# Ranking eight experts on the chip, and giving three of them 64 slots with hi and lo in one product's rows

## The chip, the cores and the metric

The kernel runs on one core of one Trainium2 chip. Its time is the device time of one execution in microseconds; the kernel before took 1813.16 us (median of 3 runs, 1811.98 to 1815.05). A core has five engines that run side by side, each through its own instructions in order: TensorE (PE in the profile; PEld are its weight loads), VectorE (DVE), ScalarE (ACT), GpSimd (POOL) and SyncE (SP), which here starts the transfers. They wait for each other by semaphores.

## The reference

The whole computation is two blocks of a network on 256 tokens of 1024 features, in float32: four mixers and a feed-forward, four mixers and a mixture of experts, a linear recurrence with feed-forward, a sparse attention with feed-forward. The change lies in the mixture of experts. Cut to what is computed:

```python
def _swiglu(h, w1, w3, w2):
    return (jax.nn.silu(h @ w1) * (h @ w3)) @ w2

def _moe_ffn(h, router, w1, w3, w2):       # h [1, 256, 1024], 8 experts of 1408 hidden features
    xt = h.reshape(T, D)
    logits = (xt @ router).astype(jnp.float32)
    top_logit, top_idx = lax.top_k(logits, TOP_K)          # TOP_K = 2
    gates = jax.nn.softmax(top_logit, axis=-1)
    ...                                    # sort by expert, evaluate blocks of rows
        yb = _swiglu(xb, w1[e], w3[e], w2[e])
    ...                                    # sum back to the tokens, times the gate
```

Of the 512 assignments the eight experts hold, for the inputs that are timed, 59, 68, 57, 76, 47, 73, 70 and 62.

## The kernel before

**Products in two parts.** Every product of float32 values is made of three passes: a value is cut into a rounded part (hi) and the rest (lo), and x·w is taken as hi·hi + lo·hi + hi·lo. For weights this is done in `piece` (L391 to L425): SP loads a piece of 128x2048 (1 MB) into one of three `raw` buffers or, while the experts run, one of `MORE` = 6 further ones (`mraw`), L401; per part of 128x1024 ScalarE casts hi (`whi`, L422) and VectorE subtracts (`wlo`, L423). The rings of `whi` and `wlo` hold three parts each (`NHL`); a part's slot comes free when TensorE has used it. Both instructions are put into the program with high priority, so that they stand ahead of other work of the engine that is written at the same place.

**The experts.** `moe` (L1163) runs once, after the second block's mixers. It makes the router's logits (L1202; the router's columns padded to 128), cuts the normalized tokens into hi and lo with tokens on partitions (`token_split`, L652), chooses two of eight per token (L1208 to L1220), counts each token's place among its expert's tokens (`pos`, L1226), and builds for two experts at a time a 0/1 matrix `G` of tokens by slots (L1272). `gather` (L1280) multiplies the tokens with it: `ehi` and `elo`, features on partitions, 128 slots for each of two experts. `slots` (L1287) makes the slot's weight and 1/rms (`gs`) and the transpose of `G` (`GT`). An expert (`expert`, L1320) has its slots on the rows of a result: chunks of 512, 512 and 384 hidden features, for each w1 and then w3 (`tmaj`, L459, 8 steps of the contraction, three products each), silu (ScalarE, L1331), product with the gate (VectorE, L1334), a transpose on TensorE (L626) and a cut into `ghi` and `glo` (L651, L652). W2 takes its pieces two steps of the contraction at a time with both halves of the features (L1373 to L1375), except in the last expert, where it goes a half of the features at a time. Then the result is weighted and cut (L1346, L1347), spread over the tokens by `GT` (scatter, L1354 and L1355, 16 products of 256 columns) and added to the residual `x` (L549).

**Order.** The program is written as a sequence; a scheduler places each engine's instructions from it, and weights' loads and splits run ahead as far as buffers allow. Experts come in the order 0 to 7 with weights at fixed addresses. The gather for the next two experts is written ahead of experts 1, 3 and 5. At the end the largest count is read into a register; if it is over 128, a second pass runs all experts on the tokens beyond. For these inputs it isn't run.

Of the kernel before, what the change touches and what calls it, by code (L numbers as in the profile page):

```python
# [8 lines left out]
F32 = mybir.dt.float32  # L9
# [52 lines left out]
class Pack:  # L62
    """Small vectors side by side in one [128, n] array."""
# [103 lines left out]
def layout(inp, phases):  # L167
    """DRAM arrays of the launch, from the inputs by name."""
# [28 lines left out]
    rt = np.zeros((P, KD, P), np.float32)  # L197
    rt[:, :, :8] = g["router"][0].reshape(KD, P, 8).transpose(1, 0, 2)
    ev.add("router", rt.reshape(P, KD * P))
# [57 lines left out]
    for j in range(2):  # L257
        w[f"c1{j}"] = _chunk_fm(g["cmp_w1_2"][j], [np.arange(256)], [8, 8])
    for e in range(8):
        w1, w3 = g["moe_w1"][0, e], g["moe_w3"][0, e]  # L260
        pc = []
        for c_ in _cols(1408, 512):
            pc += _chunk_fm(w1, [c_], [4, 4]) + _chunk_fm(w3, [c_], [4, 4])
        w[f"m13{e}"] = pc
        w[f"m2{e}"] = (_chunk_fm(g["moe_w2"][0, e], [np.arange(D)], [2, 2, 2, 2, 2, 1]) if e < 7
                      else _chunk_fm(g["moe_w2"][0, e], _cols(D, 512), [4, 4, 3]))
    for k, pieces in w.items():
# [4 lines left out]
        a["W" + k] = arr  # L272
# [3 lines left out]
# --------------------------------------------------------------------------  # L276
# the program
# --------------------------------------------------------------------------

class Prog:  # L280
# [35 lines left out]
    def keep_busy(self, n):  # L316
        """products that nobody reads, where TensorE would wait so long that its clock is halved"""
# [4 lines left out]
    def late(self):  # L322
        """the constants that are not needed at once, behind the first weights"""
# [60 lines left out]
    def prefetch(self, w):  # L384
        """start loading the first weights of the next phase, ahead of a branch"""
# [777 lines left out]
    def moe(self, after):  # L1163
# [64 lines left out]
        for q in range(2):  # L1228
            token_split(q, pts[q])
# [556 lines left out]
```

## Time and profile before

| what | value |
|---|---|
| median of 3 runs (lowest, highest) | 1813.16 us (1811.98, 1815.05) |
| profiled execution, first to last instruction | 1810.8 us |
| mean granted clock of TensorE | 0.992 |
| PE busy | 1762.0 us (97%), 11443 instructions |
| DVE busy | 1452.2 us (80%), 2129 |
| ACT busy | 1174.3 us (65%), 1716 |
| POOL busy | 91.7 us (5%), 133 |
| read from HBM | 357.92 MB, 198 GB/s over the span |
| experts' first product, last scatter | 750.34 us, 1159.7 us |

The profile is one execution. Its span runs from the first to the last instruction; the runs' times are taken apart from it and also hold what lies around the span, and the profiled execution's own time is not listed beside it. A share of the whole span mixes phases with different limits, so the rows further down are of the experts' stretch alone. A matmul's length is modelled, so the step from one start to the next tells the pace of a row of products.

### The profile page before, as it was taken

To read this page: it belongs to the slowest core of one execution; us is meant where nothing else is said; L and a number is where in the kernel's file an instruction comes from. 1 tells how busy PE (TensorE), PEld (TensorE's weight loads), DVE (VectorE), ACT (ScalarE), POOL (GpSimd) and SP (SyncE) were. 2 spreads that over 40 slices of the span, in tenths; PEclk is the share of its full clock that TensorE was granted. 3 is DMA by queue.
4 is the path that set the end of the run, shared out by engine and by line. 5 is a ranking of instruction groups with operands and counts; after the bars stand their busy time and mean duration, and the time that the engine had idled before them with its cause. 6 is when DMAs were issued, how large, how long until landed. Compare 5 with 4: busy or idle time off the path is not lost. (4 is left out here: it accounts for less than half of the span.)

```text
span 1810.8 us, 29243 instructions
## 1 busy us (share of the span) xinstructions
PE 1762.0 (97%) x11443; PEld 1566.2 (86%) x11443; DVE 1452.2 (80%) x2129; ACT 1174.3 (65%) x1716; POOL 91.7 (5%) x133
## 2 busy tenths in 40 slices
PE   8999999999999999999999999888999998999999
PEld 7888998888978899888888888788888987788888
DVE  6789787886678977789989899788887589878774
ACT  6765556554566654687887877675655477766552
POOL 1100000000110010000000000031000022000000
PEclk9999999999999999999999999998999999999999
DMA  7323555555532265789989899434555555035553
GB/s 288 130 71 117 187 187 185 186 180 190 198 132 79 100 212 176 294 315 359 354 305 353 312 360 345 162 125 150 186 186 177 197 203 177 2 101 192 193 181 126
DMA packets 53777, 360.93 MB, mean 199 GB/s; under 512 B 6112, under 2 KB 6496, under 8 KB 15744
## 3 DMA queue, kind: packets, MB, share of 16 engines
q1 hardware_dynamic: 52848, 355.57, 55.4%
q0 software_dynamic: 640, 3.38, 0.5%
q8 instruction: 92, 1.51, 0.3%
q14 instruction: 53, 0.43, 0.1%
q10 hardware_dynamic: 144, 0.04, 0.0%
HBM read 357.92 MB, written 1.05 MB: 198 GB/s over the span
## 5 line engine op out<-in xcount | busy, mean ns | idle before, releaser
L423 DVE TENSOR_TENSOR wlo<-raw,whi 128x1024 fp32r<-128x1024 f32 (+3 forms) x465 | 546.2, 1178 | 214.1 <-ACT whi L422 187.3
L422 ACT CAST whi<-raw 128x1024 fp32r<-128x1024 f32 (+3 forms) x470 | 474.8, 1013 | 357.2 <-PE lin L457 110.0
L423 DVE TENSOR_TENSOR wlo<-mraw,whi 128x1024 fp32r<-128x1024 f32 (+1 forms) x185 | 216.7, 1193 | 19.7 <-ACT whi L422 11.8
L422 ACT CAST whi<-mraw 128x1024 fp32r<-128x1024 f32 (+1 forms) x185 | 189.4, 1029 | 46.7 <-PE lin L482 25.9
L456 PE MATMUL lin<-x,whi 128*128 128x256 f32 x736 | 197.3, 289 | 6.3 <-ACT whi L420 6.3
L457 PE MATMUL lin<-x,whi 128*128 128x256 f32 x736 | 198.9, 291 | 0.0
L568 PE MATMUL lin<-x,whi 128*128 128x512 f32 x576 | 156.8, 393 | 0.0
L454 PE MATMUL lin<-x,wlo 128*128 128x256 f32 x736 | 150.9, 288 | 0.4 <-DVE wlo L423 0.3
L456 PEld LDWEIGHTS lin<-x,whi 128*128 128x128 f32 x736 | 142.9, 194 | 7.7 <-ACT whi L420 6.3
L482 PE MATMUL lin<-whi,ehi 128*128 128x512 f32 (+1 forms) x384 | 144.5, 376 | 0.0
L457 PEld LDWEIGHTS lin<-x,whi 128*128 128x128 f32 x736 | 143.1, 194 | 1.5 <-issue 0.8
L482 PE MATMUL lin<-whi,elo 128*128 128x512 f32 (+1 forms) x384 | 144.0, 375 | 0.0
L568 PE MATMUL mx<-x,whi 128*128 128x512 f32 x480 | 129.7, 392 | 0.0
L454 PEld LDWEIGHTS lin<-x,wlo 128*128 128x128 f32 x736 | 115.4, 193 | 3.8 <-issue 2.5
L568 PEld LDWEIGHTS lin<-x,whi 128*128 128x128 f32 x576 | 104.6, 189 | 15.7
L482 PE MATMUL lin<-wlo,ehi 128*128 128x512 f32 (+1 forms) x384 | 114.7, 376 | 0.0
L568 PEld LDWEIGHTS mx<-x,whi 128*128 128x128 f32 x480 | 87.3, 189 | 13.3
L577 PEld LDWEIGHTS lin<-x,wlo 128*128 128x128 f32 x576 | 86.0, 190 | 8.1
L577 PE MATMUL lin<-x,wlo 128*128 128x256 f32 x576 | 88.8, 282 | 0.0
L482 PEld LDWEIGHTS lin<-whi,ehi 128*128 128x128 f32 x384 | 72.2, 188 | 10.8 <-ACT sa L1331 0.4
L482 PEld LDWEIGHTS lin<-whi,elo 128*128 128x128 f32 x384 | 72.2, 188 | 10.0
L482 PEld LDWEIGHTS lin<-wlo,ehi 128*128 128x128 f32 x384 | 70.7, 188 | 9.9
(605 smaller groups left out, 3882.0 us busy)
## 6 DMA issues: line engine op xcount, KB each, us to landing
mraw<-Wm SPq DMA_DIRECT2D x79, 1024.0 KB, 6.5
raw<-Wf SPq DMA_DIRECT2D x60, 1024.0 KB, 4.9
raw<-Ww_gate SPq DMA_DIRECT2D x32, 1024.0 KB, 4.9
raw<-Wffn SPq DMA_DIRECT2D x30, 1024.0 KB, 4.8
raw<-Ww_in SPq DMA_DIRECT2D x25, 1024.0 KB, 5.0
raw<-Wm SPq DMA_DIRECT2D x24, 1024.0 KB, 7.4
raw<-Wm SPq DMA_DIRECT2D x24, 768.0 KB, 5.2
raw<-Ww_branch SPq DMA_DIRECT2D x8, 1024.0 KB, 4.9
```

The lines of the kernel that those rows point to most:

```text
L422: (nc.gpsimd.tensor_copy if f & 1 else nc.scalar.copy)(hi[:, :kc * n], src)
L423: (nc.gpsimd if f & 2 else nc.vector).tensor_tensor(lo[:, :kc * n], src, hi[:, :kc * n].bitcast(F32), op=ALU.subtract)
L454: nc.tensor.matmul(o, lo[:, k, fs], xhi[:, kk, :], start=False, stop=end and k == kc - 1)
L456: nc.tensor.matmul(o, hi[:, k, fs], xhi[:, kk, :], start=kk == 0 and f % 2 == 0, stop=False)
L457: nc.tensor.matmul(o, hi[:, k, fs], xlo[:, kk, :], start=False, stop=False)
L482: nc.tensor.matmul(o, (xlo if i == 2 else xhi)[:, kk, ts], (lo if i == 1 else hi)[:, k, :], start=kk + i == 0, stop=last and (k, i) == ste ...
L568: mm = lambda f=f, k=k, kk=k0 + k: nc.tensor.matmul(banks[f], hi[:, k, f * P:(f + 1) * P], x2[:, kk].rearrange("p i t -> p (i t)"), start= ...
L577: nc.tensor.matmul(banks[f][:, 0:S], lo[:, k, f * P:(f + 1) * P], x2[:, k0 + k, 0], start=False, stop=False)
```

## The change

- The 128 slots of an expert become 64 for three of the positions 1, 3 and 5 of the order in which experts are run (`CAP`). Position 0 is always expert 0. The other seven are ranked by their counts of tokens on the chip; the three with fewest go to positions 1, 3 and 5, the others by rank to 2, 4, 6 and 7 (`RANKS`).
- The ranking is a chain of small VectorE operations behind `pos`; `ordered` brings positions and gates into the new order. Seven register loads on SP give the experts' numbers, from which the addresses of w13 and W2 are made.
- A small expert (`small_expert`) holds its tokens' hi in rows 0 to 63 and lo in rows 64 to 127 of one stationary tile. `both` multiplies it with a part's hi and lo, two products where there were three, and the halves of the result are added: a copy of the lower rows on ScalarE (L1448) and an addition on VectorE (L1449). Its W2 and scatter go the same way.
- W2 of every expert goes a half of the features at a time, in pieces of 4, 4 and 3 steps; `MORE` is 7; the router has 64 columns; the gather's copies and `GT` are made per expert.
- The second pass runs if any expert has more tokens than its position has slots.

The lines taken out and put in, without those that only rename or drop comments:

```diff
-RAW, NHL, SUB, MORE = 3, 3, 1024, 6
+RAW, NHL, SUB, MORE = 3, 3, 1024, 7
+HALF = 64
+RANKS = (-1, 0, 3, 1, 4, 2, 5, 6)
+CAP = tuple(HALF if 0 <= r < 3 else P for r in RANKS)
...
-        pl = self.bank("mx").rearrange("p (t e) -> p t e", e=P)
+        pl = self.bank("mx")[:, 0:P].rearrange("p (t e) -> p t e", e=HALF)
...
+        cn = T([8], "cn")
+        nc.vector.tensor_copy(cn, pcn[:, 0:8])
+        g7, e7 = T([7, 7], "g7"), T([7, 7], "e7")
...
+        nc.vector.tensor_tensor(g7, ne, nj, op=ALU.is_gt)
+        nc.vector.tensor_tensor(e7, ne, nj, op=ALU.is_equal)
+        nc.vector.tensor_mul(e7, e7, v("jlte").rearrange("p (e j) -> p e j", e=8)[:, 1:8, 1:8])
+        nc.vector.tensor_add(g7, g7, e7)
+        rk = T([7], "rk")
+        nc.vector.tensor_reduce(rk, g7, axis=AX.X, op=ALU.add)
+        oh = T([7, 7], "oh")
+        nc.vector.tensor_tensor(oh, rk.unsqueeze(1).to_broadcast([P, 7, 7]),
+                                v("rkp").unsqueeze(2).to_broadcast([P, 7, 7]), op=ALU.is_equal)
...
+        pos_e, pos = pos, T([2, 8], "poso")
+        ordered(pos, pos_e)
+        ixf, ixi = T([7], "ixf"), T([7], "ixi", 1, I32)
...
+        order = [nc.values_load(ixi[0:1, p:p + 1], engines=(mybir.EngineType.SP,), min_val=1, max_val=7)
+                 for p in range(7)]
+        W13 = [a["Wm13"][0]] + [a["Wm13"][bass.ds(r, 1)].rearrange("a g p n -> (a g) p n") for r in order]
...
                 for d2 in range(4):
...
-                        (nc.vector.tensor_copy if e2 == 0 and src is hlo else nc.scalar.copy)(o, pt)
+                        for i in range(2):
+                            e = 2 * e2 + i
+                            dst = rows[e][0]
+                            n = slice(HALF * q, HALF * (q + 1)) if half[e] else slice(0, P)
+                            o = dst[0 if half[e] else q][:, 2 * d2:2 * d2 + 2, n]
+                            (nc.vector.tensor_copy if e2 == 0 and q else nc.scalar.copy)(o, pt[:, :, i, n])
...
-        with self.tc.If(reg > P):
-            experts(P)
+        with self.tc.If(reg > 0):
+            experts(True)
...
+    def both(self, w, first, kgroups, n, x2, sink):
...
+        for k0, kc, hi, lo in parts:
+            for i, src in enumerate((hi, lo)):
                 for k in range(kc):
...
+                    nc.tensor.matmul(bank, x2[:, k0 + k], src[:, k, :], start=k0 + k + i == 0,
+                                     stop=i == 1 and k0 + k == nk - 1)
+        sink(bank)
...
+    def small_expert(self, w13, w2, x2, gs, GT, last):
...
+        g2 = T([11, P], "ghi", 1, F32R)
+        up, dn = slice(0, HALF), slice(HALF, P)
+        rs = gs[up, 1:2]
...
+        def total(out, o):
+            nc.scalar.copy(out, o[dn])
+            nc.vector.tensor_tensor(out, o[up], out, op=ALU.add)
+        for ci, n in enumerate((512, 512, 384)):
+            sa, sb = T([512], "sa", 2)[up, :n], T([512], "sa", 2)[up, :n]
...
+            def sink_a(o):
+                total(sa, o)
+                nc.scalar.activation(sa, sa, AF.Silu, scale=rs)
...
+            def sink_b(o):
+                total(sb, o)
+                nc.vector.scalar_tensor_tensor(sa, sb, rs, sa, op0=ALU.mult, op1=ALU.mult)
...
+                self.split(g2[:, sl, up], g2[:, sl, dn], pt)
+            self.both(w13, 4 * ci, [4, 4], n, x2, sink_a)
+            self.both(w13, 4 * ci + 2, [4, 4], n, x2, sink_b)
```

In the rows below a line of the changed kernel is 5 higher than that of the same code before (L423 is L428, L626 is L631).

VectorE where the experts begin, before: cnt is the rank of a logit in its token, sel the choice, pos the places, x_1090 the tokens' lo.

```order
L1218 TENSOR_TENSOR gt_7832<-gt_7832,eq_7833 128x128
L652 TENSOR_TENSOR x_1090_7779<-mx_7801,x_1090_7779 128x512
L1219 TENSOR_REDUCE cnt_7835<-gt_7832 128x16
L652 TENSOR_TENSOR x_1090_7779<-mx_7806,x_1090_7779 128x512
L1220 TENSOR_SCALAR sel_7834<-cnt_7835 128x16
L652 TENSOR_TENSOR x_1090_7779<-mx_7815,x_1090_7779 128x512
L1226 SCALAR_TENSOR_TENSOR pos_7845<-mx_7842,sel_7834 128x16
L652 TENSOR_TENSOR x_1090_7779<-mx_7820,x_1090_7779 128x512
L1272 TENSOR_SCALAR G_7857<-pvec_7764,pos_7845 128x128 x4
L1272 TENSOR_SCALAR G_8420<-pvec_7764,pos_7845 128x128 x4
```

After, from the same place to the G that the gather waits for; wlo_8088, 8092 and 8098 are the first expert's weights, cn, g_1106, rk, oh and poso the ranking.

```order
L428 TENSOR_TENSOR wlo_8088<-mraw_8085,whi_8087 128x1024
L428 TENSOR_TENSOR wlo_8092<-mraw_8085,whi_8091 128x1024
L1223 TENSOR_TENSOR gt_7832<-gt_7832,eq_7833 128x128
L657 TENSOR_TENSOR x_1090_7779<-mx_7801,x_1090_7779 128x512
L1224 TENSOR_REDUCE cnt_7835<-gt_7832 128x16
L428 TENSOR_TENSOR wlo_8098<-mraw_8095,whi_8097 128x1024
L1225 TENSOR_SCALAR sel_7834<-cnt_7835 128x16
...
L1249 TENSOR_TENSOR oh_7860<-rk_7858,pvec_7764 128x49
L1256 TENSOR_TENSOR t_1111_7864<-oh_7860,pos_7848 128x98
L1262 TENSOR_TENSOR g_1106_7852<-oh_7860,pvec_7764 128x49
L1258 TENSOR_REDUCE poso_7862<-t_1111_7864 128x2x7
...
L1323 TENSOR_SCALAR G_7952<-pvec_7764,poso_7862 128x128
```

Three splits of weights stand between the logits and sel now, and the ranking between pos and the last G; before, three splits of the first expert stood ahead of the logits (the last is wlo_7981) and the G followed the splits of x.

TensorE at the end of w13 in the expert at position 2, before: lin_8758 is w3's last chunk, lin_8792 and lin_8793 are W2, sa_8691 the third chunk of the gated features.

```order
L482 MATMUL lin_8758<-wlo_8755,ehi_7864 128x384 x2
L1373 MATMUL lin_8792<-whi_8796,ghi_8489 128x512
L1374 MATMUL lin_8792<-wlo_8797,ghi_8489 128x512
L1375 MATMUL lin_8792<-whi_8796,glo_8490 128x512
L1373 MATMUL lin_8793<-whi_8796,ghi_8489 128x512
L1374 MATMUL lin_8793<-wlo_8797,ghi_8489 128x512
...
L1373 MATMUL lin_8792<-whi_8818,ghi_8489 128x512
L626 MATMUL mx_8784<-cst,sa_8691 128x128 x3
L1374 MATMUL lin_8792<-wlo_8819,ghi_8489 128x512
```

After; lin_9291 is w3's last chunk, lin_9354 the first half of W2, sa_9024, 9124 and 9224 the three chunks.

```order
L487 MATMUL lin_9291<-wlo_9288,ehi_8545 128x384 x2
L631 MATMUL mx_9117<-cst,sa_9024 128x128 x4
L631 MATMUL mx_9217<-cst,sa_9124 128x128 x4
L487 MATMUL lin_9354<-whi_9326,ghi_9022 128x512
L487 MATMUL lin_9354<-whi_9326,glo_9023 128x512
L487 MATMUL lin_9354<-whi_9326,ghi_9022 128x512
L487 MATMUL lin_9354<-whi_9326,glo_9023 128x512
L631 MATMUL mx_9317<-cst,sa_9224 128x128 x3
L487 MATMUL lin_9354<-wlo_9327,ghi_9022 128x512 x2
```

The transposes of the first two chunks stood among the products of the following chunks and now stand behind w13's last product.

VectorE at that place after; the L1402 rows are the products with the gate, wlo_9327 to 9341 W2's first parts.

```order
L554 TENSOR_TENSOR x<-x,mx_9018 128x512
L428 TENSOR_TENSOR wlo_9327<-mraw_9324,whi_9326 128x1024
L428 TENSOR_TENSOR wlo_9331<-mraw_9324,whi_9330 128x1024
L428 TENSOR_TENSOR wlo_9337<-mraw_9334,whi_9336 128x1024
L1402 SCALAR_TENSOR_TENSOR sa_9024<-lin_9091,gs_8544,sa_9024 128x512
L1402 SCALAR_TENSOR_TENSOR sa_9124<-lin_9191,gs_8544,sa_9124 128x512
L657 TENSOR_TENSOR glo_9023<-mx_9117,ghi_9022 128x512
L1402 SCALAR_TENSOR_TENSOR sa_9224<-lin_9291,gs_8544,sa_9224 128x384
L657 TENSOR_TENSOR glo_9023<-mx_9217,ghi_9022 128x512
L428 TENSOR_TENSOR wlo_9341<-mraw_9334,whi_9340 128x1024
L657 TENSOR_TENSOR glo_9023<-mx_9317,ghi_9022 128x384
```

The gate products of all three chunks stand behind the third split of W2; before, those of the first two stood among w13's splits.

## Rows read from the trace of the kernel before

Times are in us; "xN" counts equal instructions in a row or group, and square brackets hold the idle time before and what ended it.

**Rows 1.** Windows: stretch, length, busy PE, PEld, DVE, ACT, POOL; clock; DMA share; GB/s.
```profile
760.00:1157.00 397.00, 396.53 (x1975) 336.76 (x1974) 364.62 (x385) 314.45 (x364) 0.00 (x0) 1.00 0.88 330
861.00:962.00 101.00, 101.00 (x508) 85.97 (x507) 92.16 (x94) 80.68 (x94) 0.00 (x0) 1.00 0.91 337
840.00:860.00 20.00, 20.00 (x97) 16.60 (x97) 18.94 (x19) 15.28 (x17) 0.00 (x0) 1.00 1.00 402
744.00:747.00 3.00, 2.78 (x13) 2.81 (x14) 1.51 (x8) 0.59 (x1) 0.00 (x0) 0.50 0.99 421
1190.00:1200.00 10.00, 7.62 (x43) 6.97 (x41) 9.54 (x12) 6.46 (x14) 5.00 (x3) 0.83 0.31 105
1070.00:1080.00 10.00, 10.00 (x47) 8.13 (x47) 9.84 (x11) 8.18 (x10) 0.00 (x0) 1.00 0.98 350
```

**Rows 2.** Timeline of SP's queue: start us, length us, what, count.
```profile
735.15 4.40 SPq L401 DMA_DIRECT2D mraw<-Wm  x6
917.35 14.18 SPq L401 DMA_DIRECT2D mraw<-Wm  x6
1020.01 14.17 SPq L401 DMA_DIRECT2D mraw<-Wm  x6
```

**Rows 3.** Timeline of PE: products of 512 and of 256 columns; transposes between.
```profile
1140.42 0.40 PE L482 MATMUL lin<-whi,glo 128*128 128x512 f32 x1
1141.07 0.55 PE L626 MATMUL mx<-cst,sa 128*128 128x128 f32 x3 [0.25 <-DVE sa L1334]
1142.77 0.39 PE L482 MATMUL lin<-whi,ghi 128*128 128x512 f32 x1
1143.00 0.40 PE L482 MATMUL lin<-whi,glo 128*128 128x512 f32 x1
1152.03 0.28 PE L1354 MATMUL mx<-GT,yhi 128*128 128x256 f32 x1
1152.14 0.40 PE L1355 MATMUL mx<-GT,ylo 128*128 128x256 f32 x2
```

**Rows 4.** Groups of DVE's instructions, 760 to 1157: busy us, mean ns.
```profile
L423 DVE TENSOR_TENSOR wlo<-mraw,whi 128x1024 fp32r<-128x1024 f32 x166 | 199.8, 1222 | 17.4 <-ACT whi L422 9.5 <-ACT elo L1283 0.8
L423 DVE TENSOR_TENSOR wlo<-raw,whi 128x768 fp32r<-128x768 f32 x48 | 45.0, 956 | 3.3 <-PE lin L482 1.5 <-ACT whi L422 0.8
L549 DVE TENSOR_TENSOR x<-x,mx 128x512 f32<-128x512 f32 x30 | 20.3, 679 | 0.0
L1334 DVE SCALAR_TENSOR_TENSOR sa<-lin,gs,sa 128x512 f32<-128x512 f32 x16 | 12.0, 748 | 1.2 <-ACT sa L1331 1.0
```

**Rows 5.** Timeline of DVE: splits back to back.
```profile
1143.66 6.64 DVE L423 TENSOR_TENSOR wlo<-mraw,whi 128x1024 fp32r<-128x1024 f32 x6
```

**Rows 6.** Groups of ACT's instructions, the same stretch.
```profile
L422 ACT CAST whi<-mraw 128x1024 fp32r<-128x1024 f32 x164 | 171.9, 1053 | 40.6 <-PE lin L1375 20.0 <-PE lin L482 19.8 <-DVE wlo L423 0.3
L1283 ACT CAST ehi<-mx 128x512 fp32r<-128x512 f32 x12 | 7.3, 606 | 0.0
```

**Rows 7.** Timeline of DVE, PEld, ACT and PE where the experts begin.
```profile
739.39 0.17 DVE L1208 COPY lg<-mx 128x16 f32<-128x16 f32 x1
742.25 0.16 DVE L1220 TENSOR_SCALAR sel<-cnt 128x16 bf16<-128x16 f32 x1
743.60 1.64 DVE L1272 TENSOR_SCALAR G<-pvec,pos 128x128 fp32r<-128x128 f32 x8
734.97 3.65 PEld L1202 LDWEIGHTS mx<-pvec,x 128*128 128x128 f32 x32
738.66 1.69 ACT L1184 ACTIVATE ehi<-x,vec 128x256 f32<-128x256 f32 x4
740.25 2.00 ACT L651 CAST x<-mx 128x512 fp32r<-128x512 f32 x4
744.22 5.42 PE L1280 MATMUL mx<-G,x 128*128 128x256 f32 x32 [1.54 <-DVE G L1272]
```

**Rows 8.** Tile mosti: its register load on SP, ns.
```profile
L1315 SPq TENSOR_LOAD <-mosti x1: 471/471/471, 750.9 to 750.9; - x1
```

More of the change, by code (lines that the diff above doesn't have):

```diff
@@ L1176, in moe @@
         nc.gpsimd.memset(one, 1.0)
-        xg = T([KD, S], "ehi", 2)
+        xg = T([KD, S], "y")
         h2 = self.g([2, 2, D], "x2", 1, F32R)
@@ L1224, in moe @@
         nc.tensor.matmul(pp[:, 8:16], one, sel[:, 0], start=False, stop=True)
+        pcn = self.bank("mx")
+        for tb in range(2):
+            nc.tensor.matmul(pcn[:, 0:8], one, sel[:, tb], start=tb == 0, stop=tb == 1)
         pos = T([2, 8], "pos")
@@ L1250, in longest @@
         def longest():
-            pcn = self.bank("mx")
-            for tb in range(2):
-                nc.tensor.matmul(pcn[:, 0:8], one, sel[:, tb], start=tb == 0, stop=tb == 1)
+            no, t = T([8], "no"), T([7, 7], "g7")
+            nc.vector.tensor_copy(no[:, 0:1], cn[:, 0:1])
+            nc.vector.tensor_tensor(t, oh, nj, op=ALU.mult)
+            nc.vector.tensor_reduce(no[:, 1:8], t, axis=AX.X, op=ALU.add)
+            nc.vector.tensor_tensor(no, no, v("cap"), op=ALU.subtract)
@@ L1305, in experts @@
             for e in range(8):
-                if e % 2 == 1 and e < 7:
+                if rest and e and e % 2 == 0:
+                    slots(e // 2, gather(e // 2))
+                if not rest and e % 2 == 1 and e < 7:
                     slots(e // 2 + 1, gather(e // 2 + 1))
-                ehi, elo, gs, GT = rows[e // 2]
-                i = e % 2
-                self.expert(e, ehi[:, :, i], elo[:, :, i], gs[:, i], GT[:, i])
-        experts(0)
+                (self.small_expert if half[e] else self.expert)(W13[e], W2[e], *rows[e], e == 7)
+        experts(False)
         self.prefetch(after)
@@ L1315, in moe, with scatter, expert @@
         reg = nc.values_load(mosti[0:1, 0:1], min_val=0, max_val=S)
-        with self.tc.If(reg > P):
-            experts(P)
+        with self.tc.If(reg > 0):
+            experts(True)
         self.more, self.own = 0, False
-    def expert(self, e, ehi, elo, gs, GT):
+    def scatter(self, j, parts, GT):
+        po = self.bank("mx").rearrange("p (d t) -> p d t", d=2)
+        for i in range(2):
+            ds = slice((2 * j + i) * P, (2 * j + i + 1) * P)
+            for n, y in enumerate(parts):
+                self.nc.tensor.matmul(po[:, i], y[:, ds], GT, start=n == 0, stop=n == len(parts) - 1)
+        self.resid(j, po)
+    def expert(self, w13, w2, x2, gs, GT, last):
         nc = self.nc
         T = lambda shape, tag, bufs=1, dt=F32: self.t(list(shape), tag, bufs, dt)
-        w13, w2 = self.a[f"Wm13{e}"], self.a[f"Wm2{e}"]
+        ehi, elo = x2
         ghi, glo = T([11, P], "ghi", 1, F32R), T([11, P], "glo", 1, F32R)
@@ L1376, in expert, with sink @@
-        for b in range(2):
-            scale(b, banks[b])
-        for j in range(4):
-            scatter(j)
+        yy = T([2, D], "y", 1, F32R)
+        for b in range(2):
+            def sink(t, o, b=b):
+                ns = slice(512 * b, 512 * (b + 1))
+                nc.scalar.activation(yy[:, 0, ns], o, AF.Copy, scale=gs[:, 0:1])
+                nc.vector.scalar_tensor_tensor(yy[:, 1, ns], o, gs[:, 0:1], yy[:, 0, ns].bitcast(F32),
+                                               op0=ALU.mult, op1=ALU.subtract)
+                for j in (2 * b, 2 * b + 1):
+                    self.scatter(j, (yy[:, 0], yy[:, 1]), GT)
+            self.tmaj(w2, 3 * b, [4, 4, 3], 512, ghi, glo, 1, sink, late=True)
```

145 lines of the change are left out of this document (83 added, 62 removed).

## The prediction, made before the change was run

> **What bounds the kernel now.** I read the busy time by stretch first. Over the experts TensorE is busy 396.53 of 397 us, VectorE 364.62 and ScalarE 314.45, and the transfers hold a share of 0.88 [rows 1]. So TensorE sets the pace, but in the pair of experts at 861:962 VectorE is busy 92.16 of 101 us: it would take over after a saving of 9%. Next, the timeline of SP's queue gives the period: the same group of six loads comes again every two experts, at 917.35 and 1020.01, so a pair takes 102.7 us [rows 2], of which TensorE's own work is about 101.0. Then I read the prices. One product of 512 columns follows another after 0.23 us, one of 256 after 0.12 [rows 3]; one of 384 I take at three quarters of 0.23, 0.17. VectorE's split of 128x1024 has a mean of 1.222 us [rows 4], but six in a row take 6.64 us, 1.107 each [rows 5]: where the next is ready, about 9% of the duration overlaps. Last, the start: the logits are copied at 739.39, the one-hot rows G begin at 743.60, and the gather's products wait 1.54 us for them and begin at 744.22 [rows 7].
>
> **TensorE's saving.** A small expert drops one product in three: in w13 32 of 512 columns (7.4 us) and 16 of 384 (2.7), in W2 22 of 512 (5.1), and in the scatter 8 of 256 (1.0). That is 16.2 us, 48.6 for three experts, if nothing else were in the way.
>
> **VectorE becomes the pace of the small experts.** The weights are split as before, whatever the number of slots: 26 splits of 1024 columns, 8 of 768 and 2 of 512 per expert. Back to back (0.906 of the means 1.222, 0.956 and 0.68 [rows 4, 5]) that is 28.8 + 6.9 + 1.2 = 36.9 us. A full expert adds three products with the gate (about 2.1 by the mean of 0.748), three splits of ghi (1.9), two of y (1.5) and four residual adds (2.7 by 0.679), 8.2 us, or 7.5 back to back: 44.4. A small expert adds eight totals besides (six of 512 columns and two of 384, 5.2 us by 0.679), halves the splits of g2 and builds four G for the next pair: 36.9 + 11.5 + 1.0 = 49.4. Half of the partitions save nothing, since I price by the columns per partition; no row here has 64 partitions, and if half of the rows did halve the time, the totals, gate and y would give back 4 us.
>
> ScalarE comes close to the same: 36 casts at 1.053 or less (35 us; 33 if they overlap as its copies in the start do, four in 2.00 us against 0.606 apiece [rows 6, 7]), eight copies for the totals (about 4.4), silu, y and g2 (4.4), and the gather's sixteen copies, smaller than the eight at 0.606 but with the same start-up (about 5): 47 to 49 us. TensorE would need about 36, the pair's gather included. So a small expert lasts what VectorE lasts, with about 1 us for hand-overs from ScalarE, the six ring slots of hi and lo (three each) being too few to absorb more. Those slots are full when a full expert ends, which takes three splits (3.3 us) off the small one: 49.4 + 1.0 - 3.3 = 47.1. That VectorE can run so full, beside a busy ScalarE, is seen at 1070:1080: 9.84 of 10 us with ScalarE at 8.18 [rows 1].
>
> **The full experts.** TensorE's work in one is 30.2 (w13) + 15.2 (W2) + 1.9 (scatter) + 1.3 (transposes) = 48.6. But in the new order the transposes of two chunks no longer stand inside the products of the next chunks: all three groups come at the end of w13, and on VectorE three splits of W2 stand ahead of the three gate products. The third of these needs ring slots that w13's last products free. From their end I count a cast (1.0), a split (1.1), a gate product (0.7), the transposes (0.5), a cast of ghi (0.6) and its lo: W2 starts about 3.7 us late, 0.9 of it the transposes' own work, so 2.8 is lost. The kernel before shows the mild form at its last expert: transposes of one chunk between W2's first products, at 1141.07 after a product at 1140.42, steady pace from 1142.77 on [rows 3], about 1 us. A full expert then lasts 48.6 + 2.8 = 51.4 at most, and 50.9 if part of the transposes' wait is used. VectorE needs 44.4 + 3.3 for filling the ring again, so it is not in the way. Pair: 47.1 + 50.9 = 98.0 against 102.7: -4.7, for three pairs -14 us. Bounds: VectorE packed without hand-overs and the late transposes at the 1 us of the last expert, 94.5 (-25); everything handed over singly, 102.7 or a little above (0 to +4).
>
> **The start.** Between the logits and the last G needed by the gather, VectorE gets three splits of weights (1.23 each, about 3.7), one of them between count and sel, their casts on ScalarE standing behind eight activations that end at 740.35 [rows 7]; then about fourteen small operations of the ranking at the 0.2 us that small ones have here, and G for positions 0 and 1. By that chain: splits end about 743.8, sel 745.7, ranking and four G's 751.2. The gather begins about 7 us later than 744.22. Bounds: 5 if the splits are hidden in waits that stand there anyway, 9 if each small operation costs 0.3. Nothing covers it: TensorE has no product left to do. The logits' 64 columns instead of 128 give nothing back, for 32 weight loads take 3.65 of the 3.73 us either way [rows 7]. The gather would restart at the low clock, 0.50 at 744:747 [rows 1], as it does now. Behind the ranking SP has seven register loads (0.471 each [rows 8], about 3.5 us with the address work) before any weights of positions 1 to 7; weights of position 0 are staged by then (the last six pieces go out from 735.15 [rows 2]) and are worth over 20 us of products, so SP is not late. Transfers: 17.3 MB per expert are 43 us at the 402 GB/s of the saturated stretch [rows 1], 86 per pair, below 98. One more staging buffer, W2 by halves of the features (same pieces, bytes and products) and the per-expert copies of GT are costed at nothing: the first two move no instruction that TensorE waits for, the last hides on ScalarE in the small expert, and costs its 0.3 each if ScalarE should turn out to be the pace.
>
> **The sum.** -14 + 7 = -7. The profiled execution spans 1810.8 us; the median of the runs, 1813.16, lies 2.4 above it, for what is outside the first and the last instruction, and this stays. 1813.2 - 7 = 1806.
>
> [...]
>
> **The rivals.**
> - VectorE packs fully. For it: 9.84 of 10 us at 1070:1080; against it: a split waits for its cast and the ring is short. 94.5 a pair, -25 + 7 = -18: 1795. Chance 0.15.
> - TensorE stays the bound, VectorE's work being hidden. -48.6 + 7: about 1772. Against it: 92.16 of 101 already, and the totals come on top. Chance 0.03.
> - Slower: VectorE's instructions in the small experts are released one by one, by casts that ScalarE delivers late among the totals' and gather's copies, so each costs its single duration: 26 x 1.222 + 8 x 0.956 + 2 x 0.68 + 12.7 + 1.0 = 54.5. With the late transposes, 54.5 + 50.9 - 3.3 = 102.1, or 103 with hand-overs: the pairs win nothing, and only the start is left, +7 (to +10): 1820. It decides as soon as a small expert lasts over 49.5 us. For it: ScalarE at 47 to 49 us is as full as VectorE. Chance 0.27.
> - TensorE is fed at three quarters in the small experts and its clock falls, as at 1190:1200 (7.62 busy of 10 us, clock 0.83 [rows 1]). Products there at 0.83 would still fit under VectorE's time; only at half clock would a small expert take 70 us: +60 in all, 1866. Chance 0.03.
> - The change doesn't do what it says: one of the three holds over 64 tokens and all eight experts run again, +400. The three fewest of this input's seven hold 47, 57 and 62 tokens, the most is 76. Chance 0.01.
>
> My forecast holds 0.51.
>
> **How the numbers follow.** About 0.2% (3.6 us) is what a measurement can tell from no change. Of the forecast's 0.51 (pairs between 96 and 100, so -14 to +1), 0.36 lies below -3.6, 0.14 within 3.6, 0.01 above; of the slower case 0.05 is within. Faster 0.36 + 0.15 + 0.03 = 0.54, same 0.19, slower 0.27. The range from 1791 to 1822 holds the first case, most of the packed one and most of the slower one; the likeliest one's own range is 1799 to 1814.
>
> **What would show it.** Right: a period of about 98 us between the same loads two experts apart; in small experts VectorE busy over 95% and TensorE idle about 10 us, released by VectorE's wlo; gather's first product near 751; TensorE idle about 3 us ahead of the transposes at the end of w13 in full experts; clock 1.00. Wrong: a period of 102 or more (hand-overs eat the gain), a gather that starts by 747, TensorE idle behind a late load in position 1, or products of a second pass behind the last scatter.

## The result, and the profile after

The changed kernel takes 1833.37 us (median of 4 runs, 1832.83 to 1833.88) against 1814.1 of the kernel before in the same session: ratio 1.0108, interval 1.0094 to 1.0122. The forecast was 1806 in a range that ended at 1822, so the prediction is wrong in its sign and outside its range. The profiled execution spans 1831.1 us against 1810.8, 20.3 more, with a mean granted clock of 0.981 against 0.992.

The table cuts the experts at the first product of w13 of each position (the last cut is the end of W2 at position 7), for both kernels and the experiments. Pairs are one small and one full expert (in e1, and before, two full ones).

| kernel | first product | position 0 | 1+2 | 3+4 | 5+6 | 7 | from there to the end |
|---|---|---|---|---|---|---|---|
| before | 750.34 | 48.3 | 102.6 | 102.8 | 102.6 | 50.8 | 653.2 |
| changed | 754.51 | 54.7 | 105.5 | 105.6 | 105.7 | 49.5 | 655.5 |
| e1, all with 128 slots | 756.60 | 54.9 | 105.3 | 105.1 | 103.4 | 49.9 | 655.9 |
| e2, gates and transposes first | 755.88 | 53.0 | 97.9 | 102.6 | 105.9 | 50.9 | 657.3 |
| e3, one lo in four on GpSimd | 756.20 | 57.7 | 118.5 | 113.7 | 113.7 | 54.2 | 657.1 |
| e4, first gates first | 754.54 | 49.6 | 106.0 | 105.9 | 104.4 | 50.0 | 654.6 |
| e5, splits in written order | 754.02 | 49.2 | 101.1 | 100.9 | 101.0 | 51.8 | 658.7 |
| e6, no ranking | 753.24 | 50.1 | 109.7 | 106.2 | 108.8 | 49.8 | 654.0 |
| e7, MORE 6 | 752.25 | 52.2 | 106.6 | 106.1 | 107.0 | 49.2 | 655.3 |
| e8, e5 + e4 + e7 | 754.06 | 49.2 | 101.1 | 100.9 | 105.3 | 51.8 | 659.6 |
| e9, written order mended | 751.68 | 49.2 | 101.1 | 101.0 | 103.7 | 52.0 | 655.6 |
| e10, halves summed by TensorE | 752.27 | 49.2 | 96.0 | 102.0 | 104.4 | 52.0 | 654.4 |
| e11, as e10 with rings of 4 | 756.03 | 49.1 | 95.0 | 103.6 | 104.3 | 52.1 | 653.4 |
| e12, as e10 by priorities | 754.01 | 49.4 | 96.6 | 101.9 | 103.0 | 51.3 | 655.1 |

Of the 20.3 us, 4.2 come at the start, 6.4 in position 0, 8.7 in three pairs that should have won 14, and 2.3 behind the experts; position 7 gives back 1.3.

The windows of the changed kernel (columns as in [rows 1]): position 0, the first small expert, the first full one, and the last two once more, cut where w13 ends.

```profile
754.51:809.26 54.75, 52.10 (x240) 43.80 (x240) 45.05 (x62) 42.02 (x51) 0.00 (x0) 0.94 0.90 329
809.26:859.43 50.17, 43.12 (x196) 30.81 (x194) 46.00 (x56) 42.68 (x68) 0.00 (x0) 0.93 0.90 330
859.43:914.72 55.29, 52.08 (x243) 43.42 (x243) 50.81 (x55) 41.47 (x49) 0.00 (x0) 0.97 0.90 331
809.30:838.60 29.30, 29.03 (x145) 21.88 (x143) 28.33 (x31) 28.53 (x48) 0.00 (x0) 1.00 0.90 327
838.60:859.40 20.80, 14.02 (x51) 8.90 (x51) 17.64 (x26) 14.08 (x20) 0.00 (x0) 0.84 0.89 334
859.40:892.00 32.60, 32.60 (x157) 27.79 (x156) 32.24 (x34) 27.85 (x32) 0.00 (x0) 1.00 0.94 340
892.00:914.70 22.70, 19.49 (x86) 15.62 (x86) 18.60 (x22) 13.63 (x17) 0.00 (x0) 0.92 0.84 318
```

TensorE is idle for 10.3 us in a pair in which it was never idle before, and nearly all of it lies behind w13's last product, in the small and the full expert alike. VectorE is not full there either (17.64 of 20.80, 18.60 of 22.70): this is a wait in the order, not a lack of throughput. Nor is it the loads: TensorE waits for none among the experts. The same pair of the kernel before:

```profile
798.68:852.40 53.72, 53.72 (x279) 45.91 (x278) 47.98 (x53) 43.26 (x53) 0.00 (x0) 1.00 0.86 320
852.40:901.32 48.92, 48.92 (x239) 41.44 (x238) 46.67 (x48) 38.81 (x44) 0.00 (x0) 1.00 0.95 354
```

TensorE at that place of the changed kernel (the row's bracket is the idle time and its releaser), first small, then full; [rows 3] has the mild form that the prediction scaled from.

```profile
842.09 0.66 PE L1463 MATMUL mx<-cst,sa 64*128 64x64 f32 x4 [3.53 <-DVE sa L1459]
843.71 1.22 PE L1434 MATMUL lin<-whi,ghi 128*128 128x512 f32 x2 [0.97 <-DVE ghi L657]
...
895.22 1.94 PE L631 MATMUL mx<-cst,sa 128*128 128x128 f32 x8 [3.21 <-DVE sa L1402]
896.98 0.80 PE L487 MATMUL lin<-whi,ghi 128*128 128x512 f32 x1
897.70 0.79 PE L487 MATMUL lin<-whi,glo 128*128 128x512 f32 x1
```

And VectorE ahead of the full expert's row:

```profile
890.92 3.49 DVE L428 TENSOR_TENSOR wlo<-mraw,whi 128x1024 fp32r<-128x1024 f32 x3
894.32 1.40 DVE L1402 SCALAR_TENSOR_TENSOR sa<-lin,gs,sa 128x512 f32<-128x512 f32 x2
896.96 0.69 DVE L657 TENSOR_TENSOR glo<-mx,ghi 128x512 fp32r<-128x512 f32 x1 [1.23 <-ACT ghi L656]
```

The three W2 splits get their ring slots from w13's last products and stand ahead of the gates of chunks that had long been computed, as the order said. Behind the idle 3.2 us the granted clock is 0.50: the eight transposes there have a mean of 424 ns, against 278 among the experts before, and the first two products take 0.80 and 0.79 us, against 0.39 and 0.40 [rows 3]. The same clock is found in the small expert behind its 3.53 us:

```profile
842.00:846.00 4.00, 2.94 (x11) 1.94 (x12) 3.09 (x8) 3.11 (x5) 0.00 (x0) 0.50 1.02 430
895.20:898.30 3.10, 3.08 (x11) 2.35 (x12) 1.87 (x4) 1.54 (x3) 0.00 (x0) 0.50 1.01 425
```

The prediction spoke of this wait in full experts only. The single durations are those of [rows 4] (groups of DVE, 760 to 1170), and the totals on 64 partitions (677 ns) cost what the residual adds on 128 do (679 [rows 4]):

```profile
L428 DVE TENSOR_TENSOR wlo<-mraw,whi 128x1024 fp32r<-128x1024 f32 x136 | 161.1, 1221 | 17.6 <-ACT whi L427 15.8 <-PE lin L1434 0.5
L1449 DVE TENSOR_TENSOR sa<-lin,sa 64x512 f32<-64x512 f32 x18 | 12.0, 677 | 1.5 <-ACT sa L1448 1.3
```

SP's loads [rows 2] no longer come at an even period; the table's cuts are TensorE's.

The start (VectorE; answers [rows 7]), and the gather on TensorE:

```profile
737.95 0.17 DVE L1213 COPY lg<-mx 128x16 f32<-128x16 f32 x1 [0.63 <-PE mx L1207]
739.17 2.36 DVE L428 TENSOR_TENSOR wlo<-mraw,whi 128x1024 fp32r<-128x1024 f32 x2 [0.19 <-ACT whi L427]
742.50 1.23 DVE L428 TENSOR_TENSOR wlo<-mraw,whi 128x1024 fp32r<-128x1024 f32 x1
743.64 0.17 DVE L1225 TENSOR_SCALAR sel<-cnt 128x16 bf16<-128x16 f32 x1
747.53 0.25 DVE L1258 TENSOR_REDUCE poso<-t 128x14 f32<-128x98 f32 x1
748.02 0.16 DVE L1264 CAST ixi<-ixf 128x7 int32<-128x7 f32 x1
749.25 0.28 DVE L1323 TENSOR_SCALAR G<-pvec,poso 128x128 fp32r<-128x128 f32 x1
```
```profile
748.25 5.62 PE L1337 MATMUL mx<-G,x 128*128 128x256 f32 x32 [3.60 <-DVE ixi L1264]
```

From the logits to sel it is 5.69 us, 2.8 more than before, where 3.5 was worked out; the logits themselves come 1.44 us earlier. The chain from sel to the last G takes 5.9 us, and the gather starts at 748.25, 1.3 before the last G is written.

In position 0 it is the gates that are late. ScalarE (small steps; the casts between are left out) and TensorE:

```profile
759.49 0.30 ACT L1280 ACTIVATE gate<-gate,rcol 128x8 f32<-128x8 f32 x1
763.52 0.29 ACT L1280 ACTIVATE gate<-gate,rcol 128x8 f32<-128x8 f32 x1
778.30 1.28 ACT L1399 ACT_TABLE_LOAD   x1
779.59 1.26 ACT L1399 ACTIVATE sa<-lin,gs 128x512 f32<-128x512 f32 x2
```
```profile
780.33 0.69 PE L487 MATMUL lin<-whi,ehi 128*128 128x384 f32 x1 [2.55 <-ACT sa L1399]
780.82 0.52 PE L487 MATMUL lin<-whi,elo 128*128 128x384 f32 x1
...
786.15 0.35 PE L487 MATMUL lin<-whi,elo 128*128 128x384 f32 x1
786.33 0.34 PE L487 MATMUL lin<-whi,ehi 128*128 128x384 f32 x1
```

Between the gates' exponentials and the first silu stand eleven small steps on VectorE, most behind a split (768.87 to 776.85; the three that make gateo are new and last 2.8 from first to last, two splits among them). Two finished chunks wait for silu, and TensorE stands for 2.55 us until silu has read the first of them; then products of 384 columns follow one another after 0.32 us until 786, where the granted clock is 0.51, and after 0.18 behind it. Before, the first silu began at 773.17, 22.8 us behind the first product and not 25.1, and there was no wait.

The 2.3 us behind the experts arise at one wait in the attention, 3.87 us before and 5.94 after:

```profile
1555.47 1.75 PE L1767 MATMUL lin<-kz,qT 128*128 128x272 f32 x4 [5.94 <-ACT p L1784]
```

That code is not touched, and the instructions of TensorE, VectorE and ScalarE behind the experts stand, by names and shapes, in the same order in both traces. What differs is the clock. The products ahead of the wait and those behind it, before and after:

```profile
1528.50:1533.80 5.30, 5.28 (x20) 4.24 (x20) 5.09 (x21) 1.58 (x2) 0.54 (x1) 0.68 0.26 104
1537.70:1541.20 3.50, 3.46 (x21) 2.88 (x22) 3.29 (x18) 2.44 (x11) 0.00 (x0) 1.00 0.00 0
1545.80:1549.50 3.70, 3.63 (x20) 3.00 (x20) 3.46 (x17) 1.30 (x2) 0.59 (x1) 1.00 0.50 210
1555.40:1558.90 3.50, 3.43 (x10) 2.83 (x11) 2.33 (x12) 2.43 (x11) 0.00 (x0) 0.50 0.01 2
```

Before, the products ahead of the wait ran slowly, where the wait hid it; after, they are done sooner, the wait is longer by that and ends no later, and the half clock falls on the products behind it, where nothing hides it. The longer wait (5.35 to 5.96) is in every experiment but e11, which has 3.87, the clock at 1.00 behind it, and takes 653.4 behind the experts, as before. What moves the fall of the clock is not shown.

### The profile page after: what moved, and what is told of

It is laid out like the page before. It is cut to its first block, busy times and chain, and to the rows that moved or that the text cites. A ratio compares the mean times of both kernels' runs of the same rounds, so it can differ in the third digit from the quotient of the medians.

```text
span 1831.1 us, 29256 instructions
## 1 busy us (share of the span) xinstructions
PE 1743.5 (95%) x11209; PEld 1530.1 (84%) x11209; DVE 1462.3 (80%) x2189; ACT 1182.7 (65%) x1779; POOL 87.7 (5%) x133
## 3 DMA queue, kind: packets, MB, share of 16 engines
q1 hardware_dynamic: 52848, 355.57, 54.5%
## 5 line engine op out<-in xcount | busy, mean ns | idle before, releaser
L428 DVE TENSOR_TENSOR wlo<-raw,whi 128x1024 fp32r<-128x1024 f32 (+3 forms) x457 | 540.0, 1190 | 208.5 <-ACT whi L427 183.7
L428 DVE TENSOR_TENSOR wlo<-mraw,whi 128x1024 fp32r<-128x1024 f32 (+1 forms) x200 | 217.7, 1127 | 23.0 <-ACT whi L427 18.5
L582 PEld LDWEIGHTS mx<-x,wlo 128*128 128x128 f32 x480 | 71.6, 190 | 6.7
L487 PE MATMUL lin<-whi,ehi 128*128 128x512 f32 (+1 forms) x192 | 72.6, 378 | 2.6 <-ACT sa L1399 2.6
L582 PE MATMUL mx<-x,wlo 128*128 128x256 f32 x480 | 74.0, 282 | 0.0
L487 PE MATMUL lin<-whi,x 128*128 128x512 f32 (+1 forms) x256 | 72.9, 364 | 0.1
L487 PE MATMUL lin<-whi,elo 128*128 128x512 f32 (+1 forms) x192 | 72.3, 376 | 0.0
L573 PE MATMUL mx<-g,whi 128*128 128x512 f32 x264 | 68.3, 392 | 0.0
```

The costliest lines, as they stand in the source:

```text
L428: (nc.gpsimd if f & 2 else nc.vector).tensor_tensor(lo[:, :kc * n], src, hi[:, :kc * n].bitcast(F32), op=ALU.subtract)
L487: nc.tensor.matmul(o, (xlo if i == 2 else xhi)[:, kk, ts], (lo if i == 1 else hi)[:, k, :], start=kk + i == 0, stop=last and (k, i) == ste ...
L573: mm = lambda f=f, k=k, kk=k0 + k: nc.tensor.matmul(banks[f], hi[:, k, f * P:(f + 1) * P], x2[:, kk].rearrange("p i t -> p (i t)"), start= ...
L582: nc.tensor.matmul(banks[f][:, 0:S], lo[:, k, f * P:(f + 1) * P], x2[:, k0 + k, 0], start=False, stop=False)
```

## The experiments

Each edit is against the changed kernel unless it says otherwise; a ratio is to the kernel before, timed in the same session.

**e1_allfull: are the small experts the cost?**
```diff
-CAP = tuple(HALF if 0 <= r < 3 else P for r in RANKS)
+CAP = tuple(P for r in RANKS)
```


> All eight positions have 128 slots; ranking, register loads, W2 by halves and seven staging buffers stay. Theory A (the full experts' late gate products come from VectorE work that small experts leave behind): no idle time of TensorE over 1 us at the change from w13 to W2, every expert 49 to 54 us as before, the start 5 us and the first expert 6 us late as in the changed kernel: 1822 to 1828 us. Rival B (W2 by halves and its order alone make them late): idle times of 3 us and the low clock behind them stay in most experts: 1840 us or more.

Measured 1831.33, ratio 1.0098 (1.0082 to 1.0115), between the ranges of both theories: without one small expert the loss is as large, within the noise. The full experts at positions 2 and 4 lost nothing, and the gates of their first chunks stand among w13's splits again:

```profile
867.43:916.79 49.36, 49.36 (x239) 41.28 (x238) 46.40 (x48) 38.88 (x46) 0.00 (x0) 1.00 0.94 346
891.18 0.75 DVE L1402 SCALAR_TENSOR_TENSOR sa<-lin,gs,sa 128x512 f32<-128x512 f32 x1
```

So a full expert loses its 6 us only behind a small one. At positions 1 and 3 the small one is 5.7 and 5.5 shorter than the full one that stands there in e1 (55.9 and 55.7): the two nearly cancel. What remains in e1 is the start (6.3), position 0 (6.6), 5.7 in the pairs, whose experts with the gather last 54.1 to 55.9 against 53.7 to 53.9 before, and the 2.7 behind the experts. What makes those experts longer is not shown.

**e2_prio: the gates and transposes ahead of the splits.**
```diff
+                with self.tc.high_priority(offset=OFF + 1500):
                     (silu; gate product, transposes, split of g)
```


> Totals, silu, gate products, transposes and splits of the experts get a higher priority than the splits of weights. Theory A: where they come early the idle time of 3.2 us and the low clock (2.3 us) go; in the order this happens fully at position 6 and partly at 2 and 4, not in the small experts: 1815 to 1826 us. Rival C (VectorE's amount of work is the bound wherever the gate products stand): waits move to wlo, within 4 us of 1833.

Measured 1826.29, ratio 1.0073. The first pair lasts 97.9, the predicted 98.0 (by luck: 49.5 and 48.5, where 47.1 and 50.9 were forecast), with full experts of 48.5 at positions 2 and 4. The later pairs do not follow (positions 3 and 5 take 54.0 and 54.1): at position 3 the gather and the scatter now come between w13's last product (933.99) and the first transpose (944.53), and wait 2.25 us themselves. The mechanism of the full expert's loss is shown, the gain only once.

**e3_pool4: VectorE's load, one lo in four to GpSimd.**
```diff
-HOW = dict(rec=
+HOW = dict(moe="0002" * 72, rec=      # the string is written out
```


> GpSimd subtracts the lo of one part in four of the experts' weights (2.5 us each where the kernel before does it elsewhere, against 1.1 to 1.2 on VectorE); VectorE loses about 10 us of work per expert. Theory A and C alike: idle times at the change from w13 to W2 shrink below 1.5 us, a pair of small and full takes 96 to 99 us: 1795 to 1812 us. Rival D (the three ring slots are the limit): TensorE waits for GpSimd's parts, 1833 us or more.

Measured 1872.76, ratio 1.0333 (1.0316 to 1.035). Groups of splits by line and engine (busy us, mean ns):

```profile
L428 DVE TENSOR_TENSOR wlo<-mraw,whi 128x1024 fp32r<-128x1024 f32 x95 | 137.3, 1472 | 15.2 <-ACT whi L427 14.7
L428 POOL TENSOR_TENSOR wlo<-mraw,whi 128x1024 fp32r<-128x1024 f32 x35 | 94.4, 2697 | 258.4 <-ACT whi L427 193.5 <-PE lin L487 27.4 <-DMA mraw<-Wm 23.0
```
```profile
PE lin L1434 <- POOL wlo L428: 16.1, 18, 1.2
```

The split on GpSimd takes 2.70 us and TensorE waits for it; and beside it VectorE's own split takes 1.47 us where it took 1.22 [rows 4]. Over the experts VectorE is busy for 381.8 us, against 379.3 in the changed kernel: nothing of its load was relieved. Theories A and C miss; TensorE waits for GpSimd's parts as rival D said, but whether three ring slots are the reason is not told apart. The run does not decide whether VectorE's load is the bound.

**e4_gate: the first gates and slots ahead.**
```diff
+                with self.tc.high_priority(offset=OFF + 1500):
                     weights()
...
+            with self.tc.high_priority(offset=OFF + 1500):
+                slots(0, G)
```


> Only the gates' computation and the first slots get a higher priority. Theory: the first expert lost 6 us to a silu that waited for the gates behind splits of weights (idle 2.5 us, then the low clock); with the gates early it takes 49 to 50 us instead of 54.75: 1827 to 1829 us. Rival: the first expert is slow for another reason: 1832 to 1834 us.

Measured 1828.57, ratio 1.0085; position 0 takes 49.6 and not 54.7, and the first silu begins at 767.59. Confirmed: the late gates cost 5.2 us.

**e5_order: the splits at their written place.** `OFF` is what lets splits overtake; here it is 0 from position 0 on. It also stayed 0 in the phases behind the experts, which costs about 3 us there (658.7 in the table).
```diff
-            with self.tc.high_priority(offset=OFF):
+            with self.tc.high_priority(offset=getattr(self, "off", OFF)):
...
+            self.off = 0
```


> From the first expert on, the splits of weights keep their place in the written order instead of a high priority, so that gate products, transposes and scatter come where they are written (in the order the transposes stand among the next chunk's products at every position but 5). Theory A2 (small experts win 5.5 us each, and the late gate products and transposes, made late by the splits' priority, give it back in the full expert behind): full experts 48.5 to 49.5 us, small ones 48 to 50.5, the first still 54.75: 1813 to 1819 us. Rival C (VectorE's amount of work is the bound wherever things stand): 1829 us or more, with waits for wlo in place of those for the gate products.

Measured 1820.07, ratio 1.0036 (1.0022 to 1.0051), 1 us above the theory's range; position 0, which was to stay at 54.75, is 49.2. The first small and full expert, cut here behind the last product of W2, because four products of the full one stand ahead of it (by the table's cut they last 49.1 and 52.0; the pair is the same):

```profile
803.20:855.60 52.40, 46.10 (x208) 31.03 (x206) 49.78 (x62) 46.29 (x72) 0.00 (x0) 1.00 0.89 329
855.60:904.30 48.70, 47.99 (x229) 40.18 (x230) 46.69 (x50) 38.29 (x45) 0.00 (x0) 1.00 0.94 360
```

The waits of 3 us behind w13 are gone, the full expert is at 48.7, and the small one lasts 52.4 with VectorE busy for 49.78 of them, at a clock of 1.00; of TensorE's 5.7 us of idle time there 4.9 are ended by wlo. This is the bound that the prediction named: VectorE sets the small expert, and a pair wins 1.5 us, not 4.7.

**e6_norank: no ranking on the chip.** The experts are stored in the order that the ranking gives for this input; the chain behind `pos` and the register loads are left out.
```diff
-        nc.vector.tensor_tensor(g7, ne, nj, op=ALU.is_gt)
...
-        W13 = [a["Wm13"][0]] + [a["Wm13"][bass.ds(r, 1)].rearrange("a g p n -> (a g) p n") for r in order]
+        W13 = [a["Wm13"][p] for p in range(8)]
```


> The order of the experts that the ranking finds for these inputs is fixed beforehand in the layout of router and weights: no ranking, no register loads. Theory: the ranking costs 1.9 us between the places and the last G, and its products with the gates part of the first expert's wait for them: first product at 752 to 753 us instead of 754.5, 1828 to 1831 us. Rival E (the register loads and addresses that depend on registers hold up the weights of the later experts): gain of 8 us or more, 1825 us or less, with the periods of the experts shorter.

Measured 1834.29 (1833.54 to 1835.73). A miss: 1828 to 1831 was expected. The gather starts at 746.32, 1.9 us earlier, the first product comes 1.3 earlier, and position 0, without the steps that make gateo, takes 50.1 and not 54.7. But the pairs take 7.9 more in all, and nothing is won: the run prices the ranking at the start, not in the whole.

**e7_more6: fewer splits ahead of the ranking.**
```diff
-RAW, NHL, SUB, MORE = 3, 3, 1024, 7
+RAW, NHL, SUB, MORE = 3, 3, 1024, 6
```


> Six staging buffers instead of seven, so that the experts' first piece falls into the raw ring as in the kernel before, and its three splits stand ahead of the logits again. Theory: the gather's first product comes 3.4 us earlier (744.5 to 745.5 instead of 748.25) and nothing else changes: 1829 to 1831 us. Rival: splits ahead of the logits hold these up just as long: within 1 us of 1833.

Measured 1831.0, with the gather at 746.18, 2.1 us earlier where 3.4 was expected, and the first product 2.3 us earlier. The total is in the range, but something else did change: position 0 takes 2.6 less and the pairs 2.9 more.

**e8_order_gate_more6: e5, e4 and e7 together.**

> The written order of the first run of this call, the gates' priority that took 4.8 us off, and six staging buffers. If the parts add: 1833.3 - 16 - 4.8 - 3 = 1809 to 1812 us, about the kernel before. Theory A2: pairs of 97.5 to 99.5 us against 102.7, first expert 49.5, start 2 us late: 1803 to 1810. Rival C: 1820 or more.

Measured 1821.42, ratio 1.0039. A miss, at the rival's total: the parts do not add. Position 0 is already mended by e5 (49.2), the first product comes at 754.06 though the gather starts at 746.60, and pair 5+6 takes 105.3.

**e9_order_all: e5 and e7, `OFF` put back behind the experts, position 7 in the usual buffers.**
```diff
-                        tags = ("ex2", "ex2") if e == 7 and not rest else ("ehi", "elo")
+                        tags = ("ehi", "elo")
...
+        self.off = OFF
```


> As the run with the written order, but the splits' priority comes back behind the second pass (in that run it stayed away for all later phases), six staging buffers, and the last expert's tokens lie in the tiles of the full ones, so that position 5 also keeps the written order. Theory A3 (a small expert lasts what VectorE's work in it lasts, 52.4 us there against 53.8 before; a full one 48.7): experts 401 to 405 us, 1813 to 1817 us in all, about the kernel before. Rival: VectorE has slack and the rest is hand-overs: small experts under 50 us, 1808 or less.

Measured 1817.78, ratio 1.0026 (1.0015 to 1.0036). The start comes back to 1.3 us of before and the side effect of e5 is gone. The pairs 1+2 and 3+4 are as in e5, but 5+6 takes 103.7, and 4.8 us are left to the kernel before, just over the theory's range.

**e10_sum_on_pe: the halves added by TensorE.** On top of e9. ScalarE copies all 128 rows, scaled; the transposes multiply by two identities one above the other, which adds the halves; W2's halves go through the scatter, two products each. VectorE loses eight totals and ScalarE some copies (over the experts 15.9 and 7.9 us less than in e9); the `sa` tiles get four buffers instead of two.
```diff
-                total(sb, o)
-                nc.vector.scalar_tensor_tensor(sa, sb, rs, sa, op0=ALU.mult, op1=ALU.mult)
+                nc.scalar.activation(sb, o, AF.Copy, scale=rs)
...
+                        nc.tensor.matmul(pt[:, w, HALF * j:HALF * (j + 1)], s_[:, j * P:(j + 1) * P], self.twice,
+                                         start=True, stop=True)
+                nc.scalar.activation(sg, pt[:, 0], AF.Silu)
+                nc.vector.tensor_mul(sg, sg, pt[:, 1])
```


> The run before it, and VectorE's work in the small experts is cut: upper and lower halves are added by TensorE in the transposes (products with two identities on top of each other) and, for W2, in the scatter (two products again), where VectorE added totals and made the gate product on 512 columns; gate products have 256. That is six totals (3.9 us), 0.8 of gate products and two totals of W2 (1.35) less, 6.0 us per small expert on VectorE, about 1 us on ScalarE; TensorE gets some 3 us more. Theory A3: small experts 46 to 47.5 us, 15 to 18 us less than the run before it: 1797 to 1801 us. Rival F (ScalarE's casts and the ring of three set the pace): small experts 50 us or more, 1808 us or more.

Measured 1812.39, ratio 0.9993 (0.9984 to 1.0002): 21 us better than the changed kernel, level with the one before, and far above the theory's 1797 to 1801. Positions 1 to 4, cut as in e5:

```profile
801.42:848.51 47.09, 45.27 (x243) 36.36 (x241) 44.65 (x54) 43.17 (x69) 0.00 (x0) 1.00 0.89 344
848.51:897.39 48.88, 48.88 (x238) 41.25 (x236) 46.49 (x49) 38.84 (x46) 0.00 (x0) 1.00 0.98 371
897.39:947.49 50.10, 46.55 (x241) 35.84 (x240) 43.92 (x50) 43.27 (x69) 0.00 (x0) 1.00 0.89 335
947.49:999.42 51.93, 50.38 (x238) 41.23 (x237) 46.60 (x49) 37.80 (x45) 0.00 (x0) 1.00 0.94 342
```

With 5.1 us less on VectorE than in e5 the first small expert is 5.3 us shorter (the pair 5.1), which agrees with the bound from the other side; ScalarE's 3.1 us less are not told apart from it. The later positions have the same work and take 3 us more, and VectorE is not what holds them: at position 3 it is idle for 6.2 us. ScalarE's waits there:

```profile
ACT ghi L656 <- PE mx L631: 8.9, 6, 2.1
```

It takes its steps in order, and the cast of ghi stands at its head until the transposes come.

**e11_ring4: are rings of three too short?** e10 with rings of four (`moe=1` in `DEEP`, `MORE` 5, two `sa`).

> The run before it with four ring slots for hi and lo instead of three, five staging buffers instead of six and two buffers for the gate tiles. If hand-overs between ScalarE and VectorE cost in the small experts (rival F): 2 us or more less per small expert. Theory A3: within 2 us of the run before it, or up to 6 us slower where five staging buffers are too few for the transfers.

Measured 1816.93, ratio 1.002. Position 1 takes 46.8 and 2 48.3, cut as in e5, but 3 to 6 are no shorter than in e10 and the start is 4 us later. Longer rings do not help them here, though the five staging buffers and the `sa` tiles were changed with them.

**e12_all_prio: e10's sum, by priorities instead of the written order.** The splits keep `OFF`; gates, transposes, gather, slots and scatter get `OFF + 1500`.

> Theory: the sum of the halves on TensorE takes VectorE's load off the small experts (47 to 49 us, as seen at position 1 of the kernel that does this in the program's order), and the full experts last 48.5 to 49 as soon as their gates and transposes are issued early; here these, the gather, the slots and the scatter are put ahead by priority while the splits keep the place that they have in the changed kernel. Then positions 1 to 6 last about 48 each, position 0 49.5, the start stays 3 to 4 us late, and the total is 1803 to 1809. Rival: ScalarE takes its small steps in the written order, stands waiting for TensorE as it did from position 3 on in the kernel in the program's order (4.4 us at a time), the positions from 3 on last 50 to 52, and the total is 1811 to 1816.

Measured 1812.89, ratio 0.9998 (0.9989 to 1.0007). The rival's total, and ScalarE stands waiting for the transposes as the rival said (4.5 us at position 4). Positions 1 and 2 take 46.5 and 50.1, then 50.5 and 51.4:

```profile
899.98:950.47 50.49, 47.40 (x241) 37.08 (x240) 44.10 (x50) 43.25 (x69) 0.00 (x0) 0.97 0.90 329
950.47:1001.85 51.38, 50.13 (x238) 41.37 (x237) 46.38 (x49) 37.89 (x45) 0.00 (x0) 1.00 0.94 344
```

TensorE has no idle stretch over 1.1 us left among the experts; the loss is in many short ones. The first pair of 95 to 97 was not had three times over in any order tried. Why the later positions differ from the first stays open, and so no version beats the kernel before.

## Why the prediction was wrong

The forecast was -7 us and +20.3 came: 22.7 of the difference is in the three pairs (-14 forecast, +8.7 measured), 6.4 in position 0 and 2.3 behind the experts, which had no term; the start was 2.8 less than forecast, and position 7 gave back 1.3. The steps that failed are the price of the order behind w13, the credit of the small expert with VectorE's best-case price, and the two terms left at nothing.

- **The full expert.** "W2 starts about 3.7 us late ... 2.8 is lost." It starts 5.0 late (892.01 to 896.98), and the expert lasts 55.3, not 50.9. The mechanism was right (e1: without it 49.4; e2 and e5: 48.5 to 48.7), its size was not: the count left out that ScalarE's and VectorE's steps wait for one another (1.23 us for ghi alone), and that TensorE comes back at a clock of 0.50, with transposes of 424 ns instead of 278 and first products of 0.80 us instead of 0.40. Another 0.9 or so are four W2 products of the small expert that fall behind the cut.
- **The small expert.** The forecast gave 47.1, of which -3.3 was credit for full ring slots. VectorE's 49.4 is near e5's 49.78, but by that cut only: over the pair 93.8 was worked out and 96.5 measured. The credit is not seen, and the hand-overs cost 2.6, not 1: 52.4. In the changed kernel itself it lasts 50.2, with part of its splits left to the full expert (50.81 of VectorE's time there, against 44.4 worked out), and with the wait behind w13, which the prediction looked for in full experts alone.
- **VectorE's full expert.** 44.4 by the six splits back to back [rows 5]; measured 46.4 to 46.7 wherever it is undisturbed (before, e1, e5, e10). That row was the best case of the trace, not its mean, and the pair before, with VectorE at 94.65 us, already said so. A pair needs 96.5 (e5) against 94.65 before: the change takes TensorE's busy time from 102.6 to 94.1 (e5, short waits among the products included) and VectorE's up by 1.8, so there was never more than 6 to win with VectorE never idle, and 1.5 in fact.
- **Position 0.** No term at all. `ordered` was followed for the places, up to the gather, and not for the gates, up to the first silu; this was put at nothing without a reason, and measured 6.4, of which 5.2 come back in e4.
- **The start.** +7 worked out; the first product is 4.2 later. Taken out alone, the ranking gives back 1.3 (e6) and the seventh staging buffer, costed at nothing, 2.3 (e7). The lower bound of 5 was nearest: the logits came 1.4 earlier, and the gather did not wait for the last G.
- **Behind the experts.** +2.3 in code that the diff does not touch, costed at nothing: the half clock falls on other products. What decides that is not shown, so this part may be bad luck.
- **The rivals.** "Slower", 1820, is on the right side, but its mechanism is not what happened: the small experts did not reach 54.5, and the pairs lost at an order. Packing fully and TensorE as the bound are refuted by e5, an overflow by the experts running once. The clock fell to 0.50, but for a few us behind long waits (the windows of 4.0 and 3.1 us above; over all experts it is 0.96); that rival's 1866 should, by its own +60 on 1813, have been about 1873. The means of the single split are 1.219 and 1.221 after, and three in a row take 3.49, 1.163 each, between that and the 1.107 used.

## What to carry to other kernels

When one engine's work is cut by a third, add up every other engine's busy time over the same stretch first, from the windows and not from its best row: here VectorE held 94.65 of 102.6 us, and the change gave it more. Then read the order at each point where the next stage waits for the last small steps, and count what stands ahead of them on each in-order engine, in every kind of stage and in the first one too. A saving that shortens one stage can be lost in the next through the order alone.

## What was not expected of the hardware

- VectorE was slower with GpSimd at work beside it (e3): its split of 1024 goes from 1.22 us to 1.47 (staged parts) and 1.61 (raw ones), while GpSimd's takes 2.70 to 2.75. Its gate products on 64x512 go from 739 ns to 1293; its residual adds stay at 680 and the totals at 677. Why is not shown.
- Half the partitions saved nothing on VectorE here, which the prediction took without a row: 64x512 additions take 677 ns (above), 128x512 ones 679 [rows 4].
- The half clock can fall where a wait hides it: in the attention 0.50 cost nothing before the change (1529 to 1532) on the products ahead of a wait of 3.87 us, and 2.3 us on those behind one of 5.94.
